# First block: the outgoing products of the second group of chunks by seven products for eight, a row of constants loaded later, casts placed behind copies, and two changes of places

## The chip, the cores and the metric

The kernel runs on one core of one Trainium2 chip. The metric is the time of one execution on the device in microseconds (us), smaller is better. The core has a matrix engine (PE), a vector engine (DVE), a scalar engine (ACT), a general engine (POOL, used here to issue DMAs that add to what lies in memory) and SyncE (SP, used to issue plain DMAs). A profile of one execution gives the start and duration of each engine's instructions.

## The reference

One layer of an encoder, 512 tokens of 1024 channels in fp32. Two SwiGLU blocks stand around a mixer:

```python
h = modulate(rmsnorm(x, norm_ffn1), sh1, sc1)
x = x + 0.5 * g1 * swiglu(h, w_ffn1_in, w_ffn1_out)      # first block
...                                                       # mixer: window attention and differential attention
h = modulate(rmsnorm(x, norm_ffn2), sh3, sc3)
x = x + 0.5 * g3 * swiglu(h, w_ffn2_in, w_ffn2_out)      # second block

def swiglu(h, w_in, w_out):
    gate, up = jnp.split(h @ w_in, 2, axis=-1)
    return (jax.nn.silu(gate) * up) @ w_out
```

The hidden width is 2816. The nine shifts, scales and gates (`sh1` ... `g3`) are 72 columns of 128 values, each a product of `silu(c)` with a part of `w_mod`; the kernel calls them columns of the modulation.

## The kernel before

**Layout.** The residual `x` is held as 8 tiles `x[m]` of 128 channels x 512 tokens. The hidden width is 22 chunks of 128, or 11 pairs `p` of two chunks. A product in fp32 is made of three matmuls: high part by high part, high by low, low by high. `split_from` makes the two parts: a cast on ACT (the high part) and a subtraction on DVE (the low part, line 189). Weights arrive by DMA in `raw` or `u4` buffers and are split into a place of two large tiles, `high` and `low`. `high_low` gives the place: five places in turn, each with an offset in words, the aside (16 for `ASIDE`, -8 for `FIRST`), so that an aside moves where in its place a weight begins.

**Two ways to multiply.** `mm3` (lines 173 to 175) makes plain products, 512 tokens wide in the outgoing products of the first block. A `Unit` multiplies two-by-two blocks with seven products in place of eight (the scheme of Strassen and Winograd). Its seven products are called `s1`, `a11`, `a12`, `s2`, `s3`, `s4` and `a22`; each is made by `two` (lines 457 to 459) from matmuls that are 256 tokens wide, one half of the tokens. Its weight sums come from DMAs on POOL that add one block of weights onto another in the buffer (`s1` from two blocks, `s2` from `s1`, `s4` from `s2`, `s3` from `a11`). `Unit.after` copies a finished bank (ACT, line 535), adds banks onto copies (DVE, lines 537, 542 and 545) and calls `post` with each quarter of the result.

**The first block.** Pairs 0 to 2 take their input products plainly, pairs 3 to 10 are Units of depth 4 (24 matmuls to each of the seven products); `in_post1` turns their results into activations: silu on ACT, then `silu(gate) * up` on DVE (line 885), then a split. The outgoing products are taken in four groups of chunks, `CHUNKS`: 0 to 5, 6 to 11, 12 to 15, 16 to 21. When the pairs of a group are done, an `Out1` follows: for each of the 8 outputs `m` all chunks of the group, 3 matmuls of 128x512 to a chunk, and an update of `x[m]` on DVE (line 946).

**What sets the order.** The items (one product of a Unit, or one output of an `Out1`) stand in a list, and the matrix engine runs them in that order (`run_items`). An item's weights are asked for (`ASK`) and split (`MAKE`) so many items ahead. `in_order` names the products whose split is tied behind the latest copy of a bank on ACT (`issue_after(copied[0])`). Beside each item `side1` adds 0.27 to a credit, and at 1.0 one column of the modulation is loaded and reduced on DVE (line 282). SP, POOL and DVE run their instructions strictly in the order given.

**The second block** runs Units for its input and its outgoing products alike: `act_split` makes the seven operands of an outgoing Unit from a pair's activations, piece by piece beside the items. It starts with `plain` (pair 0, plain blocks `a11`, `a21`, `a12`, `a22`, in two halves of the tokens), `lead` (pair 1) and `units[2]`.

## Time and profile before

| what | us |
|---|---|
| three timed runs | 1034.28, 1035.11, 1036.36 |
| their median | 1035.11 |
| the profiled execution, its whole time | 1038.52 |
| the profiled execution, span of its trace | 1036.7 |
| first block, first matmul of pair 3 | 81.62 |
| plain outgoing products, chunks 0 to 5 | 108.90 to 141.57 |
| plain outgoing products, chunks 6 to 11 (the second group) | 179.73 to 212.41 |
| plain outgoing products, chunks 12 to 15 | 250.56 to 272.36 |
| second block, first product of a Unit | 711.30 |

Starts are on the profiled execution's own clock, from the start of its span. The whole time of that execution is 1.8 us above its span, and 3.4 us above the median of the timed runs. The profile shows each matmul with a duration of its own; since matmuls overlap, the pace of the matrix engine is read from the distance between their starts.

### The profile page before, as it was taken

Reading aid. Unit: us, or ns where it says so; the run is one execution under the profiler, and the core shown is the slowest. Engines: PE = TensorE matmul, PEld = TensorE weight load, DVE = VectorE, ACT = ScalarE, POOL = GpSimd, SP = SyncE. Lnnn points to the kernel's source line nnn. Section 1 sums busy time; section 2 is a strip of 40 time slices with the busy share of each in tenths; the row PEclk is TensorE's granted clock in tenths of the full one; section 3 lists DMA queues with packets and bytes.
Section 4 is the critical chain, followed back from the end, with each engine's and each line's share of the span. In section 5 each row is a group of like instructions: output and inputs, shape, how many; then the busy total and the mean of one; then the engine's idle time right before and its main releaser. Section 6 shows DMA issues by size and latency. Waiting matters only on the chain.

```text
span 1036.7 us, 18849 instructions
## 1 busy us (share of the span) xinstructions
PE 1030.0 (99%) x7346; PEld 950.1 (92%) x7346; DVE 788.1 (76%) x1457; ACT 583.5 (56%) x1013; POOL 162.2 (16%) x189
## 2 busy tenths in 40 slices
PE   9999999999999999999999999999999999999998
PEld 6889899899998998899888888989999999999998
DVE  6987667567797679859772688976898777877877
ACT  6754335244455343668785856525867546654553
POOL 1101110110110100543323101001112112112210
PEclk9999999999999999999999999999999999999999
DMA  9978887967884359796737934974598998999974
GB/s 358 356 222 203 234 235 215 257 157 222 236 204 149 137 214 410 232 283 137 176 79 186 267 133 153 362 242 102 103 235 183 241 223 215 221 229 214 210 156 112
DMA packets 70233, 220.39 MB, mean 213 GB/s; under 512 B 8448, under 2 KB 13184, under 8 KB 70144
## 3 DMA queue, kind: packets, MB, share of 16 engines
q1 hardware_dynamic: 47808, 146.52, 39.1%
q0 software_dynamic: 19200, 68.17, 36.0%
q10 hardware_dynamic: 3136, 4.51, 1.2%
q8 instruction: 57, 0.93, 0.3%
q14 instruction: 32, 0.26, 0.1%
HBM read 208.94 MB, written 10.23 MB: 211 GB/s over the span
## 4 chain that ended last, share of the span: by engine, by line
PE 92%; DVE 2%; DMA 2%; ACT 2%; issue 1%; POOL 0%; DVEq 0%; SPq 0%; ACTq 0%
PE acc L457 7%; PE acc L458 7%; PE acc L459 7%; PE sc L459 6%; PE sc L457 6%; PE sc L458 6%; PE sc L174 5%; PE sc L173 5%; PE sc L175 5%; PE acc L173 4%; PE acc L175 4%; PE acc L174 4%; PE tp L1279 2%; PE acc L708 2%; PE acc L1201 2%; PE acc L1200 2%
## 5 line engine op out<-in xcount | busy, mean ns | idle before, releaser
L189 ACT CAST high<-raw 128x1024 fp32r<-128x1024 f32 (+2 forms) x176 | 158.4, 914 | 152.3 <-PE sc L174 40.8
L189 DVE TENSOR_TENSOR low<-raw,high 128x1024 fp32r<-128x1024 f32 (+2 forms) x176 | 183.4, 1051 | 39.7 <-ACT high L189 38.2
L457 PE MATMUL acc<-b,high 128*128 128x256 f32 x508 | 141.1, 278 | 0.0
L458 PE MATMUL acc<-b,high 128*128 128x256 f32 x508 | 140.8, 277 | 0.1
L459 PE MATMUL acc<-b,low 128*128 128x256 f32 x508 | 140.7, 277 | 0.0
L459 PE MATMUL sc<-b,low 128*128 128x256 f32 x500 | 138.4, 277 | 0.0
L457 PE MATMUL sc<-b,high 128*128 128x256 f32 x500 | 138.4, 277 | 0.0
L458 PE MATMUL sc<-b,high 128*128 128x256 f32 x500 | 138.4, 277 | 0.0
L189 ACT CAST high<-u 128x1024 fp32r<-128x1024 f32 (+1 forms) x73 | 75.5, 1034 | 53.8 <-PE sc L174 20.2
L189 DVE TENSOR_TENSOR low<-u,high 128x1024 fp32r<-128x1024 f32 (+1 forms) x73 | 87.7, 1201 | 21.6 <-ACT high L189 19.9
L174 PE MATMUL sc<-b,high 128*128 128x512 f32 (+1 forms) x272 | 97.2, 357 | 0.3 <-DVE b L189 0.3
L173 PE MATMUL sc<-b,high 128*128 128x512 f32 (+1 forms) x272 | 97.4, 358 | 0.0
L175 PE MATMUL sc<-b,low 128*128 128x512 f32 (+1 forms) x272 | 97.0, 357 | 0.0
L457 PEld LDWEIGHTS acc<-b,high 128*128 128x128 f32 x508 | 95.6, 188 | 0.4 <-ACT f L535 0.2
L458 PEld LDWEIGHTS acc<-b,high 128*128 128x128 f32 x508 | 95.4, 188 | 0.4 <-DVE b L1895 0.3
L459 PEld LDWEIGHTS acc<-b,low 128*128 128x128 f32 x508 | 95.4, 188 | 0.0
L457 PEld LDWEIGHTS sc<-b,high 128*128 128x128 f32 x500 | 94.2, 188 | 0.0
L458 PEld LDWEIGHTS sc<-b,high 128*128 128x128 f32 x500 | 93.9, 188 | 0.0
L459 PEld LDWEIGHTS sc<-b,low 128*128 128x128 f32 x500 | 93.8, 188 | 0.0
L173 PE MATMUL acc<-b,high 128*128 128x512 f32 (+1 forms) x240 | 89.1, 371 | 0.0
L175 PE MATMUL acc<-b,low 128*128 128x512 f32 (+1 forms) x240 | 86.5, 361 | 0.0
L174 PE MATMUL acc<-b,high 128*128 128x512 f32 (+1 forms) x240 | 86.5, 360 | 0.0
(397 smaller groups left out, 2715.4 us busy)
## 6 DMA issues: line engine op xcount, KB each, us to landing
u<-w_mod SPq DMA_DIRECT2D x38, 512.0 KB, 7.8
b<-w_mod SPq DMA_DIRECT2D x32, 512.0 KB, 5.9
raw<-w2i SPq DMA_DIRECT2D x31, 512.0 KB, 5.0
u<-w2i POOLq DMA_DIRECT2D x31, 512.0 KB, 6.5
raw<-w1u SPq DMA_DIRECT2D x24, 512.0 KB, 7.0
u<-w1u POOLq DMA_DIRECT2D x24, 512.0 KB, 7.5
raw<-w1o SPq DMA_DIRECT2D x24, 384.0 KB, 4.9
raw<-w_gate SPq DMA_DIRECT2D x16, 512.0 KB, 5.2
```

Of the source, the lines that this page charges most:

```text
L173: PE.matmul(out, wh, xh, start=first, stop=False)
L174: PE.matmul(out, wh, xl, start=False, stop=False)
L175: PE.matmul(out, wl, xh, start=False, stop=last)
L189: last = S.copy(hi, src), V.tensor_tensor(lo, src, f(hi), ALU.subtract)
L457: PE.matmul(out, wh[:, s], xh, start=first and j == 0, stop=False, skip_group_check=True)
L458: PE.matmul(out, wh[:, s], xl, start=False, stop=False, skip_group_check=True)
L459: PE.matmul(out, wl[:, s], xh, start=False, stop=last and j == 1, skip_group_check=True)
L708: PE.matmul(out1[i][:, r], w[:, i * P : (i + 1) * P], h[:, r], start=first and r.start == 0, stop=last and r.stop == T, skip_group_check=True,
L1200: PE.matmul(out[t][:, 0:n], hh[k][:, ht], wh[:, o : o + n], start=k == 0, stop=False)
L1201: PE.matmul(out[t][:, 0:n], hh[k][:, ht], wl[:, o : o + n], start=False, stop=False)
L1279: PE.transpose(tp[:, j * P : (j + 1) * P], src, ident)
```

## The change

It has six parts.

1. **The second group by sevens.** `SEVEN = (1,)`: chunks 6 to 11 (pairs 3, 4, 5) are no longer multiplied by an `Out1`, but by two outgoing Units of depth 3 (`out_unit1`, outputs 0 to 3 and 4 to 7). Their weights are laid out as `w1q`, 128x768 to a block. The activations of the three pairs are turned into seven operands each by `act_split`, which moves up from the second block and serves both.
2. **The order of items.** Units 4, 5 and 6 run first; the two outgoing Units then run interleaved with unit 6, with each other and with unit 7.
3. **Columns of the modulation.** The credit of an item is 0.6 for an output of a plain group, 0.25 for a product of a Unit and 0.1 beside the items of the sevens, for 0.27 before.
4. **The row of constants** (`row`, used after the first block) is loaded beside the first item of unit 9, not early; until then its `u4` buffer is free for others.
5. **Casts behind copies.** For the Units that follow a pair of the sevens (4, 5 and 6), the splits of five products are tied behind the latest copy (`s1`, `s2`, `s3`, `s4`, `a22`), for two before.
6. **Places.** `FIRST` stays on `s2` of units 4 and 8 and goes from unit 6. In the second block `a21` and `a22` of `plain` and `a11` of `units[2]` lie at `THIRD` (48); before they lay at the ordinary aside and at `FIRST`.

```diff
+THIRD = 48
...
-EARLY, NEXT, SIDE, LATER = 3, 3, 0.27, 4
+SEVEN, RATES = (1,), (0.6, 0.25, 0.1)
+EARLY, NEXT, LATER = 3, 3, 4
...
-    row = u4(F32).rearrange("p a b -> p (a b)")[:, 0:NROW]
     freq = keep([P, HD // 2], "freq")
     small_loads = [
-        (row, a["row"].partition_broadcast(P)), (kept[0], a["pos"]), (freq, a["freq"].partition_broadcast(P)),
+        (kept[0], a["pos"]), (freq, a["freq"].partition_broadcast(P)),
     ]
...
         g = u.v["g" + c[2]]
+        if u.p in by_sevens:
+            V.tensor_tensor(g, g, v, ALU.mult)
+            return
         V.scalar_tensor_tensor(g, g, -1.0, v, ALU.mult, ALU.mult)
+        if u.p in by:
+            return
...
-        u.p, u.in_order = p, ('s2', 's4')
+        u.p, u.in_order = p, ("s2", "s4")
+        if p - 1 in by_sevens:
+            u.in_order = ("s1", "s2", "s3", "s4", "a22")
...
-        elif 2 * p in [c.start for c in CHUNKS[1:]] or p == PLAIN + 1:
+        elif 2 * p in [CHUNKS[i].stop for i in range(len(CHUNKS) - 1) if i not in SEVEN] or p == PLAIN + 1:
             u.asides = {"s2": FIRST}
...
+    def act_split(u, k):
+
+        ta, tb = f2(), f2()
+        b = {f"b{n + 1}{t + 1}": u.v[f"g{t + 1}"][:, r] for t in range(2) for n, r in enumerate(HALVES)}
+        b.update(n1=ta[:, T1], n2=ta[:, T2], t3=tb[:, T1], t4=tb[:, T2])
+        for o in ("n1", "b11", "b21", "n2", "b22", "t3", "t4"):
+            if o in SUMS:
+                sub(b[o], *(b[q] for q in SUMS[o]), o in NEGATED)
+            act[o, k] = t = act_place()
+            split_from(*t, b[o])
+            yield
...
+    def out_unit1(part, g, odd):
+        def post(c, v, u):
+            n, t = int(c[1]) - 1, int(c[2]) - 1
+            for j in range(2):
+                m = 4 * g + 2 * n + j
...
+                w = (less if n == 0 else modv[G1])[:, m : m + 1]
+                if n == 0 and m not in negated:
+                    negated.add(m)
+                    V.tensor_scalar(w, modv[G1][:, m : m + 1], -1.0, None, ALU.mult)
+                xr = x[m][:, HALVES[t]]
+                V.scalar_tensor_tensor(xr, v[:, j * H : (j + 1) * H], w, xr, ALU.mult, ALU.add)
+
+        r = slice((part.start - PLAIN) * 2 * P, (part.stop - PLAIN) * 2 * P)
+        srcs = {q: a["w1q"][g, i][:, r] for i, q in enumerate(("a11", "a12", "a21", "a22"))}
+        u = Unit(srcs, len(part), act_operand, post, odd)
+        return u
+
+    def load_row():
+        rows.append(u4(F32).rearrange("p a b -> p (a b)")[:, 0:NROW])
+        nc.sync.dma_start(rows[0], a["row"].partition_broadcast(P))
+
+    by[-1] = lambda: (iter(()), 0, load_row)
...
+        for v, nxt in zip(order, order[1:] + [None]):
+            n = RATES[1 + (v.p in by_sevens or v not in units1.values())]
+            due = [v.p - 1] if v in units1.values() and v.p - 1 in by else []
+            if v is units1[NH - 2]:
+                due.append(-1)
...
+            item1(v, "s2", *due, n=n)
+            to = nxt is not None and v in units1.values() and nxt not in units1.values()
+            if nxt and not to:
+                item1(nxt, "s1", n=n)
+            item1(v, "s3", n=n)
+            item1(v, "s4", n=n)
+            if to:
+                item1(nxt, "s1", rest=True, n=n)
+            if nxt:
+                item1(nxt, "a11", n=n)
+            item1(v, "a22", n=n)
...
-    units[2].asides = {"a11": FIRST}
+    units[2].asides = {"a11": THIRD}
+    plain.asides = {"a21": THIRD, "a22": THIRD}
```

**On the matrix engine.** Before, unit 6's `a12` (bank `op`) was followed by the `Out1` of the second group, whose matmuls are 512 wide (bank `sc`, the first of 8 outputs). The names are output bank, then tokens operand and weights:

```order
L459 MATMUL op_165_1698<-b8_13_98,low_94 128x256
L457 MATMUL op_165_1698<-b8_13_98,high_87 128x256
L458 MATMUL op_165_1698<-b8_15_100,high_87 128x256
L459 MATMUL op_165_1698<-b8_13_98,low_94 128x256
L173 MATMUL sc_167_1729<-b8_122_983,high_87 128x512
L174 MATMUL sc_167_1729<-b8_122_983,high_87 128x512
L175 MATMUL sc_167_1729<-b8_122_983,low_94 128x512
```

Now unit 6 goes on. Shown are the last three matmuls of its `s2` (bank `acc_167`), six of its `s4` (bank `acc_163`), and the first three of its `s3`, which adds to the bank of `s2` again:

```order
L461 MATMUL acc_167_1663<-b8_103_732,high_87 128x256
L462 MATMUL acc_167_1663<-b8_103_732,high_87 128x256
L463 MATMUL acc_167_1663<-b8_103_732,low_94 128x256
L461 MATMUL acc_163_1566<-b8_13_98,high_87 128x256
L462 MATMUL acc_163_1566<-b8_15_100,high_87 128x256
L463 MATMUL acc_163_1566<-b8_13_98,low_94 128x256
L461 MATMUL acc_163_1566<-b8_13_98,high_87 128x256
L462 MATMUL acc_163_1566<-b8_15_100,high_87 128x256
L463 MATMUL acc_163_1566<-b8_13_98,low_94 128x256
L461 MATMUL acc_167_1663<-b8_104_739,high_87 128x256
L462 MATMUL acc_167_1663<-b8_104_739,high_87 128x256
L463 MATMUL acc_167_1663<-b8_104_739,low_94 128x256
```

In the other units the 24 matmuls of the next unit's `s1` stand between `s2` and `s3`; at this one place (`to` in the code) only six matmuls of `s4` stand there, and the copy of bank `acc_167` has to be made within them. The same arrangement stands in both kernels in unit 10, which has no next unit.

**On ACT**, before, the copy of unit 6's `a11` (from `acc_162`) stood ahead of the plain group, with the casts of that group's weights (`raw` to `high`, 768 wide) behind it:

```order
L877 ACTIVATE f2_157_1542<-f2_157_1542 128x512
L189 CAST b8_160_1630<-f2_157_1542 128x2x256
L535 COPY f2_163_1665<-acc_162_1640 128x512
L189 CAST high_87<-raw_161_1635 128x768
L189 CAST high_87<-raw_164_1696 128x768
```

Now the copy for unit 6's `s3` (`f2_175` from `acc_167`) stands behind a silu, a cast of an activation's operand and a cast of an outgoing Unit's weights:

```order
L880 ACTIVATE f2_168_1688<-f2_168_1688 128x512
L193 CAST b8_176_1798<-f2_171_1731 128x256
L193 CAST high_87<-raw_165_1626 128x768
L539 COPY f2_175_1793<-acc_167_1663 128x512
L193 CAST high_87<-raw_169_1693 128x1024
```

What moved: ahead of the copy there is now a cast of weights, which waits for its weights' DMA.

**On DVE**, before, each output of the plain group brought one split of weights (`low`, 768 wide) and one update of `x` (512 wide):

```order
L189 TENSOR_TENSOR low_94<-raw_168_1751,high_87 128x768
L189 TENSOR_TENSOR low_94<-raw_170_1778,high_87 128x768
L946 SCALAR_TENSOR_TENSOR x_3_78<-sc_167_1729,mod2_90,x_3_78 128x512
L189 TENSOR_TENSOR low_94<-raw_173_1805,high_87 128x768
L946 SCALAR_TENSOR_TENSOR x_4_79<-sc_169_1756,mod2_90,x_4_79 128x512
L189 TENSOR_TENSOR low_94<-raw_175_1829,high_87 128x768
```

Now a product of the outgoing Units brings a split of the same width; each quarter of a result brings a sum of banks (L546, L541) and two updates of 256 (L992):

```order
L546 TENSOR_TENSOR f2_182_1920<-f2_182_1920,tp_185_1952 128x512
L193 TENSOR_TENSOR low_94<-raw_177_1867,high_87 128x768
L992 SCALAR_TENSOR_TENSOR x_3_78<-f2_182_1920,sm_79_572,x_3_78 128x256
L992 SCALAR_TENSOR_TENSOR x_4_79<-f2_182_1920,sm_79_572,x_4_79 128x256
L193 TENSOR_TENSOR low_94<-raw_183_1922,high_87 128x768
L193 TENSOR_TENSOR low_94<-u4_170_1728,high_87 128x768
L541 TENSOR_TENSOR f2_180_1897<-f2_180_1897,sc_181_1901 128x512
L992 SCALAR_TENSOR_TENSOR x_5_80<-f2_180_1897,mod2_90,x_5_80 128x256
L992 SCALAR_TENSOR_TENSOR x_6_81<-f2_180_1897,mod2_90,x_6_81 128x256
```

What moved: the updates of `x` are twice as many and half as wide, and sums of banks and splits of more weights stand among them. Over the program PE has 7240 rows for 7132, DVE 1448 for 1401, ACT 898 for 875 and POOL 192 for 184; SP has 330 in both. From the end of unit 10 on, the order of each engine is the same in both kernels.

185 lines of the change are left out of this document (104 added, 81 removed).

## The prediction

> **What bounds the kernel now.** I read the page first, then the waits of the matrix engine, then starts in the timeline. The page's head:
>
> ```profile
> span 1036.7 us, 18849 instructions
> PE 1030.0 (99%) x7346; PEld 950.1 (92%) x7346; DVE 788.1 (76%) x1457; ACT 583.5 (56%) x1013; POOL 162.2 (16%) x189
> PEclk9999999999999999999999999999999999999999
> PE 92%; DVE 2%; DMA 2%; ACT 2%; issue 1%; POOL 0%; DVEq 0%; SPq 0%; ACTq 0%
> ```
>
> The matrix engine is busy for 99% of the span at its full granted clock, and 92% of the chain that ended last is its work. What it waits for (longest first and last):
>
> ```profile
> PE acc L633 <- DVE sm L639: 0.9, 1, 0.9
> ...
> PE acc L708 <- ACT b L695: 0.3, 1, 0.3
> ```
>
> Columns are total, number and longest wait. There are five such rows, 2.6 us together, and none has a line of the seven-product code (gaps of some tenths show only in the starts, below). So time is saved by fewer or denser matmuls, and lost where another engine comes late. Busy time does not give a matmul's cost, since matmuls overlap; their starts do. Around the stage that is replaced:
>
> ```profile
> 179.62 0.28 PE L459 MATMUL op<-b,low 128*128 128x256 f32 x1
> 179.73 0.40 PE L173 MATMUL sc<-b,high 128*128 128x512 f32 x1
> 179.96 0.40 PE L174 MATMUL sc<-b,high 128*128 128x512 f32 x1
> ```
>
> Start, duration, instruction. The last narrow start (256 columns) is 0.11 us ahead of the next, the first wide one (512) 0.23. Over stretches, in the windows:
>
> ```profile
> 179.73:212.41 32.68, 32.68 (x147) 27.03 (x146) 17.93 (x26) 7.13 (x8) 3.52 (x4) 1.00 0.91 258
> 212.41:215.20 2.79, 2.79 (x25) 2.79 (x24) 0.75 (x1) 0.00 (x0) 0.00 (x0) 1.00 0.00 0
> 142.00:180.00 38.00, 38.00 (x336) 37.96 (x335) 28.86 (x38) 21.27 (x28) 3.50 (x4) 1.00 0.84 233
> 142.00:251.00 109.00, 109.00 (x816) 103.30 (x815) 75.77 (x100) 49.43 (x65) 11.43 (x13) 1.00 0.78 214
> 766.00:820.00 54.00, 54.00 (x462) 54.00 (x462) 46.63 (x73) 35.42 (x57) 9.17 (x11) 1.00 0.91 225
> ```
>
> After the length stand PE, PEld, DVE, ACT and POOL busy with their counts, the granted clock, the DMA share and GB/s; a count takes in the two or three matmuls that run over an edge. The first row is the whole stage that is replaced: 8 outputs x 6 chunks x 3 = 144 wide matmuls in 32.68 us, 226.9 ns each. In the third row some 335 narrow ones fill 38 us: 113.4 ns, half of it. I use 113.3.
>
> **The change, part by part.**
>
> *The sevens.* Two outgoing Units x 7 products x 3 pairs x 2 x 3 = 252 narrow matmuls, 252 x 0.1133 = 28.55 us, for 32.68: **-4.1 us**. The 24 matmuls from 212.41 to 215.20 (second row), the first after wide ones, took 2.79 us for 24 x 0.1133 = 2.72; unit 6 no longer follows wide ones: **-0.1**.
>
> *The new wait.* Unit 6's `s3` follows `s2` after only six matmuls. Unit 10 has that order in the kernel before (matrix engine, then ACT):
>
> ```profile
> 313.69 0.28 PE L458 MATMUL acc<-b,high 128*128 128x256 f32 x1
> 313.80 0.28 PE L459 MATMUL acc<-b,low 128*128 128x256 f32 x1
> 314.07 0.39 PE L457 MATMUL acc<-b,high 128*128 128x256 f32 x1
> 314.30 0.28 PE L458 MATMUL acc<-b,high 128*128 128x256 f32 x1
> 314.42 0.28 PE L459 MATMUL acc<-b,low 128*128 128x256 f32 x1
> ```
>
> ```profile
> 313.44 0.59 ACT L535 COPY f<-acc 128x512 f32<-128x512 f32 x1 [1.02 <-PE acc L459]
> ```
>
> The starts 313.80, 314.07, 314.30 are 270 and 230 ns apart for 113: 0.27 us lost to a copy that was issued at once. In unit 6 a cast of 768 stands ahead of the copy, 0.84 us by its row below; bounds are 0 (the copy lands within the six) and 0.27 + 0.84 = 1.1. I take the nearest row, **+0.3**. Behind the copy on ACT stand casts for later items, not this one.
>
> *What hides the rest.* Costs on DVE and ACT:
>
> ```profile
> L189 DVE TENSOR_TENSOR low<-raw,high 128x768 fp32r<-128x768 f32 x32 | 30.1, 953 | 9.2 <-ACT high L189 9.2
> L189 DVE TENSOR_TENSOR b<-f,b 128x256 fp32r<-128x256 f32 x71 | 27.9, 420 | 2.1 <-ACT b L189 1.6
> L189 DVE TENSOR_TENSOR b<-f,b 128x512 fp32r<-128x512 f32 x22 | 15.1, 688 | 5.2 <-ACT b L189 5.2
> L588 DVE SCALAR_TENSOR_TENSOR f<-f,f 128x256 f32<-128x256 f32 x22 | 9.2, 420 | 0.1
> L545 DVE TENSOR_TENSOR f<-f,acc 128x512 f32<-128x512 f32 x12 | 8.2, 683 | 1.8 <-PE acc L459 1.7
> L946 DVE SCALAR_TENSOR_TENSOR x<-sc,mod,x 128x512 f32<-128x512 f32 x24 | 18.0, 750 | 27.1 <-PE sc L175 27.1
> L1818 DVE SCALAR_TENSOR_TENSOR x<-f,mod,x 128x256 f32<-128x256 f32 x36 | 15.8, 481 | 0.5
> L282 DVE CUSTOM_DVE_ANT_0 u<-u,ka 128x1024 f32<-128x1024 f32 x15 | 18.2, 1218 | 0.0
> L189 ACT CAST high<-raw 128x768 fp32r<-128x768 f32 x32 | 26.0, 837 | 24.5 <-PE sc L174 11.5 <-DMA raw<-w1o 7.1 <-PE acc L458 3.2
> ```
>
> Off DVE go 8 splits of 768 (7.6), 8 updates (6.0) and 6 splits of 512 (4.1): 17.7 us. On it come 14 splits of 768 (13.3), 21 splits and 12 sums of 256 (33 x 0.420 = 13.9), 6 sums of banks (4.1) and 16 updates of 256 (7.7): 39.0. Net +21.3. The columns there are ten before, two instructions each:
>
> ```profile
> 142.00:251.00 109.00, 12.44 (x20) 1.00 0.78 214
> ```
>
> By the new rates eight remain, -2.5 (the two come later, beside stages with room). The row 142 to 251 has 75.8 us of DVE in 109; it becomes 94.6 in 105, 90%. That is close, but the row 766 to 820, which runs sevens throughout, has 46.6 of 54, 86%. ACT gets 6 casts of 768, 6 copies, and 21 casts of 256 for 6 of 512, some 13 us on 49: 60%. Both lie beside matmuls: I cost them at **0**, and in the rivals as the price if that cover goes.
>
> *Transfers.* SP's 8 loads of 384 KB become 8, POOL gets 8 more that add, in the same 105 us:
>
> ```profile
> raw<-w1u SPq DMA_DIRECT2D x24, 512.0 KB, 7.0
> u<-w1u POOLq DMA_DIRECT2D x24, 512.0 KB, 7.5
> raw<-w1o SPq DMA_DIRECT2D x24, 384.0 KB, 4.9
> ```
>
> 214 GB/s x 109 us is 23.3 MB; with 3.1 MB more in 105 us it is 252 GB/s, and the share rises from 0.78 to about 0.9, as in the row 766 to 820. **0** again.
>
> *The row of constants* is one more load in SP's row beside unit 9; behind it stand loads that are asked for six to nine products (16 to 24 us) before use and land in 7.0 us. On DVE a copy from it stands ahead of a split for unit 10; if the row is late, DVE waits up to a landing, about 7 us, against a need more than 8 us off. **0**. Its buffer is free until then, which can only help. *Casts behind copies* keep copies early in the stretch of the sevens and are part of that cover.
>
> *Places.* The narrow matmuls do not always go at 113 ns. At the start of the second block, again in windows:
>
> ```profile
> 729.69:741.00 11.31, 11.31 (x99) 11.31 (x98) 9.76 (x19) 8.79 (x16) 0.91 (x1) 1.00 0.29 46
> 741.00:743.87 2.87, 2.87 (x26) 2.87 (x25) 2.60 (x3) 2.87 (x4) 0.86 (x1) 1.00 0.02 6
> 743.87:746.68 2.81, 2.81 (x27) 2.81 (x25) 2.81 (x4) 1.68 (x4) 0.86 (x1) 1.00 0.99 163
> 746.68:765.75 19.07, 19.07 (x171) 19.02 (x169) 17.78 (x27) 13.94 (x24) 4.35 (x5) 1.00 1.01 216
> ```
>
> By the code these are `plain`'s second half (96 matmuls), `s1` of `lead` (24), `a11` of `units[2]` with `FIRST` (24), and seven more products (168): 117.8, 119.6, 117.1 and 113.5 ns each. If `THIRD` brings all to 113.3 it gives 0.43 + 0.15 + 0.09 = 0.7 us. If it runs at the slowest pace of these rows, 119.6, and leaves 117.8 behind it up to 765.75, it costs 96 x 0.0018 + 24 x 0.0025 + 168 x 0.0045 = 0.2 + 0.1 + 0.8 = 1.1. From 766 to 820 there are at most 462 in 54 us, where 54 / 0.1133 = 477 would fit: 15 fewer, 1.7 us, of which another phase at the start may be rid. So -2.4 to +1.1; both signs are open, I take **0**.
>
> Sum: -4.1 - 0.1 + 0.3 = **-3.9 us**. Against the profiled execution, 1038.5, that is 1034.6. It stands 3.4 us above the median of the timed runs; from 1035.1 it is **1031.2 us**.
>
> **A rule against it.** The rows say that one wide matmul costs two narrow ones (226.9 to 113.1). The Trainium skill, "TensorE: Matmul & The Clock Gate", section "Back-to-back issue gap", gives streams of weight load and matmul about 131 ns for 512 columns and 81 for 128; on a line between them 256 columns would be some 98, an estimate, and the stage would go from 18.9 to 24.7 us, slower by 5.8. The rows here contradict both its figures and its ratio.
>
> **The rivals.**
>
> 1. *The new wait leaves a slower pace.* From 766 on (the row above) the matmuls were slow, 54 / 460 = 117.4 ns, for as long as the window; after 314.30 the next start came 0.12 us later. If unit 6's wait does the first, 558 narrow matmuls up to the next wide stage take 4.5 ns more: 2.5 us, **1033.7**, no measurable change. For it: slow stretches exist at a granted clock of 1.00, so the clock does not undo them. Against: unit 10, the same arrangement, was back at once. Chance 0.2.
> 2. *DVE comes late in the sevens.* At 90% over 105 us it has 10 us of room, but not evenly; a column (1.2 us) ahead of a split can delay an item by as much. Two or three such waits cost 2 to 3 us: **1033.7**. Chance 0.12.
> 3. *Slower: a landing is exposed.* An outgoing Unit's `s4` weights are `s2`'s with a block added by POOL. `s2` is split four products ahead of its own, and `s4` comes three after that; at 18 x 0.1133 = 2.04 us a product, not 2.72, these seven are 14 us for a landing of 7.5, a cast and a split. If landings stretch past 14 us, each late one is waited for in full; from 6.0 us (3.9 + 0.2% of the time) the kernel is slower. One landing exposed: 1031.2 + 7.5 = **1038.7**. For it: share 0.9, 8 more adding transfers. Against: 766 to 820 runs the same chain at 0.91 and the list of waits has no DMA. Chance 0.08.
> 4. *A narrow matmul costs more than half a wide one*, because its weight load shows. Were all exposed,
>
> ```profile
> L457 PEld LDWEIGHTS acc<-b,high 128*128 128x128 f32 x508 | 95.6, 188 | 0.4 <-ACT f L535 0.2
> ```
>
> 252 x 0.188 = 47.4 us for 32.7: +14.7, **1049.8**. The rule above, of the Trainium skill, would come from such a cost. The starts at 113 speak against it: chance 0.02.
>
> **How the numbers follow.** The forecast has 0.58. The range takes in its open terms: down by 0.3 (no wait) and 2.4 (places), to 1028.5; up by rival 1 or 2 and 1.1 (places), to 1034.8. Rivals 3 and 4 stay outside. A measurement of this kernel can tell 0.2%, 2.1 us, from no change, so faster is below 1033.0: the forecast, and a part of rivals 1 and 2 where places help, 0.70. Within 0.2%: 0.20. Slower: rivals 3 and 4, 0.10.
>
> **What would show it.** In the profile after: no matmul of 512 columns between units 5 and 7, and narrow ones at 113 ns in their place; the span of the first block shorter by 3.9 us; a gap of 0.3 us behind `s2` of unit 6, and the pace behind it (rival 1); waits of PE on DVE or ACT lines in the sevens (rival 2) or on `raw<-w1q` (rival 3). The second block's start shows the places by 96 and 24 matmuls as above. It is wrong if the first block gains under 2 us, or if the time changes behind 820, where nothing is altered.

## The result and the profile after

The changed kernel takes 1045.73 us in the median of six runs (1045.16 to 1050.21), the kernel before beside it 1034.89 us (six runs, 1034.28 to 1036.36). The ratio is **1.0102, with a 95% interval of 1.0086 to 1.0117**: 1% slower, where 0.4% faster was forecast. The profiled execution of the changed kernel has a span of 1045.0 us, for 1036.7.

The page's head after the change, the same lines as shown of before:

```profile
span 1045.0 us, 19171 instructions
PE 1029.7 (99%) x7454; PEld 954.7 (91%) x7454; DVE 805.2 (77%) x1508; ACT 593.9 (57%) x1040; POOL 169.2 (16%) x197
PEclk9999999999999999999999999999999999999999
```

The matrix engine is busy for 1029.7 us, as long as before, although it was given less to do; its share still rounds to 99%. The list of its waits shows what the share hides. Columns: engine, bank and line, what was waited for, then total, number and longest in us.

```profile
PE acc L461 <- ACT f L539: 3.9, 2, 2.9
PE acc L461 <- DVE f L541: 3.1, 1, 3.1
PE acc L637 <- DVE sm L643: 0.9, 1, 0.9
PE sc L461 <- ACT f L539: 0.8, 1, 0.8
PE tp L463 <- DVE low L193: 0.6, 1, 0.6
PE acc L463 <- DVE low L193: 0.5, 1, 0.5
```

Before, no row of this list had a line of the seven-product code. Now five of the first six have (L461 and L463 are the former L457 and L459): copies of banks on ACT, a sum of banks on DVE, the splits of weights on DVE.

Windows give the place. Each row has the stretch and its length, then PE, PEld, DVE, ACT and POOL busy with counts, the granted clock, the DMA share and GB/s. First the kernel before, from the first matmul of pair 3 to the first wide one of the last group:

```profile
81.62:321.68 240.06, 240.06 (x1730) 224.80 (x1728) 172.51 (x241) 106.43 (x140) 25.79 (x30) 1.00 0.79 216
```

The changed kernel, the same stretch of the program, then the stretch around the sevens, three pieces at unit 6, and one of the second block:

```profile
80.54:328.72 248.18, 240.15 (x1837) 229.30 (x1836) 189.29 (x291) 117.45 (x167) 32.88 (x38) 0.99 0.84 224
...
142.00:251.00 109.00, 105.50 (x911) 104.90 (x910) 85.50 (x131) 59.89 (x89) 18.50 (x21) 0.98 0.89 223
...
181.00:185.80 4.80, 1.50 (x11) 1.10 (x9) 4.33 (x9) 2.92 (x8) 0.00 (x0) 1.00 0.89 246
185.80:190.30 4.50, 4.44 (x24) 4.44 (x25) 3.54 (x8) 2.05 (x4) 0.87 (x1) 0.62 0.83 259
190.30:217.50 27.20, 27.20 (x242) 27.20 (x241) 22.30 (x34) 12.94 (x19) 6.20 (x7) 1.00 0.99 236
...
766.00:820.00 54.00, 52.96 (x452) 52.76 (x451) 49.21 (x81) 37.11 (x62) 10.94 (x13) 1.00 0.89 208
```

The stretch grew by 8.12 us (248.18 - 240.06) where 3.9 less was forecast, so 12.0 us were lost in it. It began 1.08 us earlier (80.54 for 81.62), which lies ahead of what was changed on the matrix engine (in the profiles below it begins anywhere from 79.67 to 80.85), and what follows the stretch adds 1.2; -1.1 + 8.1 + 1.2 is within 0.1 of the 8.3 us between the spans.

The sevens themselves run at the pace forecast: the row from 190.30 holds 242 matmuls in 27.20 us, 240 x 0.1133. What was lost lies in two places. I measure each by the starts of the matmuls: the sum of what their distances exceed 113.3 ns (226.7 for wide ones). **At unit 6's `s3`** (178 to 192 us) it is 5.5 us: the row from 181.00 has PE busy for 1.50 of 4.80 us, and the row behind it ran at a granted clock of 0.62, with matmuls 213 ns apart for a while ("half a clock" below). **At units 8 and 9** (from the third plain group to ahead of unit 10's own wait, 273 to 320 us) it is 6.0 us. The rest of the stretch has 1.4, where the kernel before has 0.7 in all.

**Who is late at unit 6.** The timeline of ACT (start, duration, instruction, and in brackets the idle time before it and who ended it), changed kernel:

```profile
174.45 0.83 ACT L193 CAST high<-u 128x768 fp32r<-128x768 f32 x1 [5.15 <-DMA u<-w1q]
...
180.66 1.02 ACT L193 CAST b<-f 128x256 fp32r<-128x256 f32 x3 [0.94 <-DVE f L889]
183.52 0.63 ACT L880 ACTIVATE f<-f 128x512 f32<-128x512 f32 x1 [1.84 <-DVE f L546]
...
185.23 0.58 ACT L539 COPY f<-acc 128x512 f32<-128x512 f32 x1
```

The last row is the copy that `s3` waits for; `s2` had ended at 181.5, and `s3` started at 185.86. ACT had stood idle for 5.15 us, ten us earlier, for the weights of an outgoing Unit (`u<-w1q`) that nothing on PE needed yet. DVE stood behind it, and later ACT behind DVE:

```profile
175.32 0.96 DVE L193 TENSOR_TENSOR low<-u,high 128x768 fp32r<-128x768 f32 x1 [3.47 <-ACT high L193]
...
181.00 1.22 DVE L193 TENSOR_TENSOR low<-u,high 128x1024 fp32r<-128x1024 f32 x1
...
182.80 0.68 DVE L546 TENSOR_TENSOR f<-f,op 128x512 f32<-128x512 f32 x1
```

The DMA that ended ACT's 5.15 us is the one that adds on POOL. It was issued 8.8 us before that cast could start, and stood on POOL behind another adding DMA that had waited 12 us for its buffer, while SP had issued the plain load that it adds to at 149.41 already:

```profile
165.13 0.88 POOL L516 DMA_DIRECT2D raw<-w1u  x1 [12.02 <-DVE low L193]
165.68 1.23 POOL L497 DMA_DIRECT2D u<-w1q  x1
```

So three queues that run in order hand the lateness on: POOL to ACT (5.15), ACT to DVE (3.47), DVE to ACT (1.84), ACT to PE.

**Who is late at units 8 and 9.** The row of constants and the weights of unit 9's `s1` in the timeline of the changed kernel (SP, ACT and DVE):

```profile
263.39 0.47 SPq L495 DMA_DIRECT2D u<-w1u  x1
...
273.79 0.38 SPq L1003 DMA_DIRECT2D u<-row  x1
...
282.58 1.05 ACT L193 CAST high<-u 128x1024 fp32r<-128x1024 f32 x1 [4.99 <-DMA u<-w1u]
...
285.55 0.17 DVE L1257 COPY sink<-u 128x8 f32<-128x8 f32 x1 [6.70 <-DMA u<-row]
...
289.22 0.68 DVE L541 TENSOR_TENSOR f<-f,acc 128x512 f32<-128x512 f32 x1
```

and before:

```profile
255.27 0.51 SPq L491 DMA_DIRECT2D u<-w1u  x1
```

DVE waits 6.70 us for the row of constants, which landed 11.7 us after its issue; the sum L541, which frees a bank, stands behind, and PE waits 3.1 us for it. ACT meanwhile waits 4.99 us for the adding DMA of unit 9's `s1`; SP had issued the plain load below that sum at 263.39, 12.1 us after the start of the third plain group (251.25), before 4.7 us after it.

The transfers by queue from 142 to 251 us, with packets, MB and the share of 16 DMA engines' time (software_dynamic is POOL's adding DMAs, hardware_dynamic SP's loads), before:

```profile
q1 hardware_dynamic: 5190, 16.44, 41.1%
q0 software_dynamic: 1872, 6.82, 36.5%
```

and after:

```profile
q0 software_dynamic: 2962, 9.71, 52.0%
q1 hardware_dynamic: 4608, 14.42, 36.0%
```

A MB of the adding DMAs takes 52.0/9.71 = 5.4% of the stretch, one of SP's loads 36.0/14.42 = 2.5%. Without the adding DMAs (`e13_no_adds`, below) SP's loads `raw<-w1u` land after 3.6 us in the median, not 6.1. The Trainium skill, "DMA: Bandwidth & Descriptors", section "Issuing engines are not separate DMA queues", says that DMAs issued from different engines end on the same 16 DMA engines and interleave. These landings agree with it.

### The profile page after: what moved, and what is told of

Same layout as the page of the kernel before. It is cut to its first block, busy times and chain, and to the rows that moved or that the text cites. A ratio compares the mean times of both kernels' runs of the same rounds, so it can differ in the third digit from the quotient of the medians.

```text
span 1045.0 us, 19171 instructions
## 1 busy us (share of the span) xinstructions
PE 1029.7 (99%) x7454; PEld 954.7 (91%) x7454; DVE 805.2 (77%) x1508; ACT 593.9 (57%) x1040; POOL 169.2 (16%) x197
## 5 line engine op out<-in xcount | busy, mean ns | idle before, releaser
L461 PE MATMUL acc<-b,high 128*128 128x256 f32 x542 | 151.8, 280 | 7.1 <-ACT f L539 3.9
L463 PE MATMUL acc<-b,low 128*128 128x256 f32 x542 | 151.4, 279 | 0.5 <-DVE low L193 0.5
L462 PE MATMUL acc<-b,high 128*128 128x256 f32 x542 | 151.2, 279 | 0.4 <-DVE b L2010 0.4
L461 PE MATMUL sc<-b,high 128*128 128x256 f32 x534 | 148.0, 277 | 0.8 <-ACT f L539 0.8
L463 PE MATMUL sc<-b,low 128*128 128x256 f32 x534 | 147.9, 277 | 0.0
L462 PE MATMUL sc<-b,high 128*128 128x256 f32 x534 | 147.8, 277 | 0.0
L193 ACT CAST high<-u 128x1024 fp32r<-128x1024 f32 (+1 forms) x79 | 80.4, 1018 | 57.2 <-PE sc L462 12.1
L461 PEld LDWEIGHTS acc<-b,high 128*128 128x128 f32 x542 | 102.7, 189 | 8.0 <-ACT f L539 4.6
L463 PEld LDWEIGHTS acc<-b,low 128*128 128x128 f32 x542 | 102.8, 190 | 0.8 <-DVE low L193 0.7
L462 PEld LDWEIGHTS acc<-b,high 128*128 128x128 f32 x542 | 102.6, 189 | 0.7 <-DVE b L2010 0.6
L461 PEld LDWEIGHTS sc<-b,high 128*128 128x128 f32 x534 | 100.3, 188 | 1.0 <-ACT f L539 1.0
L463 PEld LDWEIGHTS sc<-b,low 128*128 128x128 f32 x534 | 100.5, 188 | 0.0
L462 PEld LDWEIGHTS sc<-b,high 128*128 128x128 f32 x534 | 100.3, 188 | 0.0
L177 PE MATMUL sc<-b,high 128*128 128x512 f32 (+1 forms) x224 | 78.7, 352 | 0.0
L178 PE MATMUL sc<-b,high 128*128 128x512 f32 (+1 forms) x224 | 78.5, 351 | 0.1
L179 PE MATMUL sc<-b,low 128*128 128x512 f32 (+1 forms) x224 | 78.4, 350 | 0.0
```

The lines of the kernel that those rows point to most:

```text
L177: PE.matmul(out, wh, xh, start=first, stop=False)
L178: PE.matmul(out, wh, xl, start=False, stop=False)
L179: PE.matmul(out, wl, xh, start=False, stop=last)
L193: last = S.copy(hi, src), V.tensor_tensor(lo, src, f(hi), ALU.subtract)
L461: PE.matmul(out, wh[:, s], xh, start=first and j == 0, stop=False, skip_group_check=True)
L462: PE.matmul(out, wh[:, s], xl, start=False, stop=False, skip_group_check=True)
```

## The experiments

The timed ratio is to the kernel before, with its 95% interval. Block is the stretch of the first block as above, and the next columns are the excess of starts at unit 6 (178 to 192 us) and at units 8 and 9 (up to unit 10's own wait); these three come from one profiled execution each, in us.

| run | median (range) | ratio (95%) | block | unit 6 | units 8, 9 |
|---|---|---|---|---|---|
| before | 1034.89 | 1 | 240.06 | 0.0 | 0.1 |
| after | 1045.73 (1045.16 to 1050.21) | 1.0102 (1.0086 to 1.0117) | 248.18 | 5.5 | 6.0 |
| e1_copy_late | 1041.09 (1039.88 to 1045.12) | 1.0054 (1.0034 to 1.0074) | 243.76 | 5.3 | 2.1 |
| e2_s4_first | 1043.13 (1040.28 to 1044.04) | 1.0059 (1.0034 to 1.0083) | 248.06 | 4.1 | 5.8 |
| e3_both | 1039.31 (1037.05 to 1044.19) | 1.0037 (1.0020 to 1.0053) | 244.08 | 1.7 | 5.3 |
| e4_places_back | 1045.88 (1044.00 to 1046.42) | 1.0087 (1.0062 to 1.0113) | 249.01 | 4.8 | 5.9 |
| e5_before_row_late | 1036.69 (1035.52 to 1040.10) | 1.0008 (0.9996 to 1.0021) | 241.36 | 0.0 | 1.4 |
| e6_out_weights_later | 1044.86 (1041.06 to 1046.27) | 1.0078 (1.0053 to 1.0103) | 250.00 | 5.2 | 5.6 |
| e7_old_rates | 1042.92 (1041.28 to 1043.10) | 1.0066 (1.0048 to 1.0083) | 243.56 | 6.7 | 0.1 |
| e8_all_four | 1041.50 (1040.93 to 1045.12) | 1.0059 (1.0036 to 1.0081) | 244.21 | 4.6 | 0.1 |
| e9_s4_split_late | 1045.66 (1044.29 to 1046.72) | 1.0088 (1.0058 to 1.0118) | 250.22 | 5.4 | 6.4 |
| e10_two_causes_gone | 1042.15 (1037.58 to 1044.49) | 1.0058 (1.0039 to 1.0077) | 244.98 | 4.2 | 2.1 |
| e11_next_s1_between | 1039.89 (1038.47 to 1042.86) | 1.0036 (1.0022 to 1.0050) | 244.21 | 0.0 | 1.8 |
| e12_all_but_sevens | 1036.71 (1034.33 to 1039.24) | 1.0009 (0.9999 to 1.0019) | 244.14 | 0.0 | 4.2 |
| e13_no_adds | 1034.02 (1032.14 to 1035.81) | 0.9988 (0.9979 to 0.9997) | 238.99 | 0.8 | 1.0 |
| e14_less_dve | 1045.16 (1043.70 to 1048.57) | 1.0101 (1.0085 to 1.0118) | 250.31 | 5.5 | 5.8 |
| e15_neither | 1031.97 (1030.88 to 1033.86) | 0.9966 (0.9955 to 0.9978) | 236.18 | 0.3 | 0.1 |
| e16_places_alone | 1035.25 (1034.79 to 1036.72) | 1.0002 (0.9994 to 1.0011) | 240.06 | 0.0 | 0.1 |
| e17_no_out_adds | 1040.43 (1038.30 to 1042.12) | 1.0039 (1.0026 to 1.0052) | 242.69 | 0.4 | 5.3 |
| e18_no_out_adds_old_rates | 1038.29 (1034.15 to 1042.19) | 1.0018 (1.0000 to 1.0037) | 240.19 | 2.6 | 1.2 |

One profile says only so much: `e2` and `e3` have the same order of work up to unit 6 and lose 4.1 and 1.7 us there, and in `e4`, `e9`, `e11`, `e12` and `e14` the profiled execution is the slowest of those timed. The block ends where the last plain group begins; the five runs with 0.25 of a column beside a plain output (`e7`, `e8`, `e10`, `e11`, `e18`) lose 1.0 to 2.3 us more right behind it, where three or four of the columns that were put off stand on DVE.

### Single waits: the copy behind the row, the order at unit 6, the places

**e1_copy_late.** The copy from the row of constants, with what follows from it, is tied behind the last split of the first block.

```diff
-    V.tensor_copy(
-        sink.rearrange("p (g k) -> p k g", k=2), row[:, ROW_SINK : ROW_SINK + 8].rearrange("p (k g) -> p k g", k=2)
-    )
+    with tc.issue_after(split[1]):
+        V.tensor_copy(
+            sink.rearrange("p (g k) -> p k g", k=2), row[:, ROW_SINK : ROW_SINK + 8].rearrange("p (k g) -> p k g", k=2)
+        )
```

> The changed kernel with one thing moved: the copy of the sink values out of the row of constants stands on DVE behind the last weight split of the first block, not in the middle of unit 8. The row is loaded at the same place. Theory (head of line: DVE stood for 6.7 us on the row, and the sum L541 that unit 8's a22 needs stood behind it): the waits of the matrix engine between 281 and 303 us, about 5 us with the slower pace behind them 6.6 us, go; 1045.7 becomes about 1039. Rival (the row's own transfer slows the weights' loads, and DVE has too little time there anyway): less than 2 us goes.

The wait of 3.1 us for the sum L541 is gone; 0.95 us at 297.4 and a pace of 118 ns behind it are left. Unit 6 is unchanged. The row still lands late (11.4 us after its issue); that DVE stood for it was the first cause of the waits at units 8 and 9. The time is 2 us above the theory's.

**e2_s4_first.** Unit 6's `s4` ahead of its `s3`, so that 24 matmuls and not six stand between `s2` and `s3`.

```diff
-            item1(v, "s3", n=n)
-            item1(v, "s4", n=n)
+            for q in ("s4", "s3") if to else ("s3", "s4"):
+                item1(v, q, n=n)
```

> The changed kernel with unit 6's s4 ahead of its s3, so that 24 matmuls (2.72 us) stand between s2 and s3 where there were six (0.68 us). Theory (the copy that s3 waits for stands on ACT behind two casts and a silu that wait for a late DVE): 2.0 of the 3.8 us of waiting go, and with a shorter idle stretch the 1.7 us at a lower granted clock behind it too; 1045.7 becomes 1042 to 1043. Rival (DVE lacks the time in the sevens as a whole): the wait comes back at the next products, 1045 or more.

Unit 6 loses 4.1 us instead of 5.5: the copy comes so late that 24 matmuls don't cover it either. The few matmuls between `s2` and `s3` are not the whole cause; they are the place where the lateness shows.

**e3_both.** Both edits together.

> Both edits together. Theory: the two waits are apart (100 us between them), so their gains add: 1045.7 - 6.6 - 3.5 = 1035 to 1036. Rival (one backlog of DVE runs through both): clearly less than the sum of the two.

Unit 6 falls to 1.7 us, and no half clock follows; the waits at units 8 and 9 return without the row: 2.6 us at 283.3, then half a clock. ACT stands 7.54 us idle there for the adding DMA of `u<-w1u`. A wait that is taken away uncovers the next one. The gains did not add up, as the theory had it: 1039.31 for 1035 to 1036.

**e4_places_back.** `a21`, `a22` of `plain` and `a11` of `units[2]` at their places of before.

```diff
-    units[2].asides = {"a11": THIRD}
-    plain.asides = {"a21": THIRD, "a22": THIRD}
+    units[2].asides = {"a11": FIRST}
```

> The changed kernel with the places at the start of the second block as before (a11 of units[2] at FIRST, a21 and a22 of plain at the ordinary aside). Theory (the places speed up plain's matmuls by 0.7 us, and a copy on ACT that waits for DVE 20 us later takes that back): no change, 1045.7 within 0.7 us, with the wait at 770 us shorter by about what the matmuls ahead of it lose. Rival (the places cost something by themselves): 1.2 us faster.

No change outside the intervals: the places carry none of the loss that can be measured.

**e5_before_row_late.** The kernel before, with the row of constants loaded beside unit 9 and nothing else.

```diff
-    row = u4(F32).rearrange("p a b -> p (a b)")[:, 0:NROW]
...
-        (row, a["row"].partition_broadcast(P)), (kept[0], a["pos"]), (freq, a["freq"].partition_broadcast(P)),
+        (kept[0], a["pos"]), (freq, a["freq"].partition_broadcast(P)),
...
+    def load_row():
+        rows.append(u4(F32).rearrange("p a b -> p (a b)")[:, 0:NROW])
+        nc.sync.dma_start(rows[0], a["row"].partition_broadcast(P))
+        side1()
```

> The kernel before with one part of the change alone: the row of constants is loaded beside the first product of unit 9. Theory (the copy from the row stands on DVE ahead of unit 8's sums and waits for the row's landing, which took 11.7 us in the changed kernel): the matrix engine waits behind the third plain group, 2 to 5 us, 1035 becomes 1037 to 1040. Rival (the row costs only together with the new rates of columns, which make the loads ahead of it late): within 1 us of before.

One wait of 1.1 us at 279 us, and a ratio that can't be told from 1. The late row is not free, but it takes the company of the other parts to cost three us.

### Moving weights and columns about

**e6_out_weights_later** splits the first outgoing Unit's `s1` weights three items ahead and not five, so that the cast on which ACT waited comes later. **e7_old_rates** loads 0.25 of a column beside a plain output and not 0.6. **e8_all_four** has e1, e2, e6 and e7 together.

```diff
+        if g == 0:
+            u.MAKE = {**Unit.MAKE, "s1": 3}
...
-SEVEN, RATES = (1,), (0.6, 0.25, 0.1)
+SEVEN, RATES = (1,), (0.25, 0.25, 0.1)
```

> The changed kernel with the split of the first outgoing Unit's s1 weights made three products ahead, not five; on ACT its cast moves from row 132 to row 136, behind a silu and a copy. Theory (ACT stood 5.2 us on the landing of that Unit's summed weights, with the silu, the activations' casts and at last the copy for unit 6's s3 behind it): the 3.8 us of waiting at 181 us shrink to 1 us or less, and the 1.7 us at a lower clock behind it go; 1045.7 becomes 1040 to 1041.5. Rival (DVE is simply full in the sevens): the wait stays above 2.5 us, 1044 or more.

> The changed kernel with 0.25 column for each output of a plain group, not 0.6 (0.25 and 0.1 elsewhere as changed). Theory (five loads of w_mod in the third plain group hold up SP ahead of unit 9's weights, whose load was issued 12 us after that group's start for 5 us before): the wait of ACT on u<-w1u at 277 us shrinks from 5.0 us to under 2, the waits of the matrix engine at 284 us and after lose 2 to 4 us; 1045.7 becomes 1042 to 1044. Rival (the row alone makes the waits): no change.

> The changed kernel with four edits: the copy from the row late, unit 6's s4 ahead of its s3, the first outgoing Unit's s1 split three products ahead, 0.25 column for each output of a plain group. Theory (the seven-product stage itself saves its 4.1 us, and all that was lost are transfers waited for at the head of in-order engines): 1031 to 1034, faster than before. Rival (DVE lacks time in the sevens): 1036 or more.

In e6 ACT no longer waits for `w1q`; it waits 3.03 us for the next weights, unit 6's own `s4`, and unit 6 loses 5.2 us as before. In e7 the waits at units 8 and 9 are gone (0.1 us): SP issued the plain load for unit 9's `s1` at 257.42, the row landed 7.5 us after its issue, and DVE waited 1.31 us for it. So columns between SP's loads are part of that cause. But unit 6 loses 6.7 us, and one more wait of 1.3 us comes at 346.6, where columns that were put off are now due. In e8 none of the four edits gets rid of unit 6's wait: ACT stands 4.64 us for unit 6's `s4` weights.

**e9_s4_split_late** splits unit 6's `s4` one item ahead and not two. **e10_two_causes_gone** has that with e6 and e7. **e11_next_s1_between** has e6 and e7 with the first outgoing Unit's `s1` put between unit 6's `s2` and `s3`, as in every other unit.

```diff
+        if p - 1 == by_sevens[-1]:
+            u.MAKE = {**Unit.MAKE, "s4": 1}
...
-            if nxt and not to:
-                item1(nxt, "s1", n=n)
+            if nxt:
+                item1(nxt, "s1", rest=to, n=n)
...
-            if to:
-                item1(nxt, "s1", rest=True, n=n)
```

> The changed kernel with unit 6's s4 split one product ahead, not two: on ACT its cast then stands behind the copy that unit 6's s3 waits for, where it stood ahead of it. Theory (that cast waits for the landing of s2's weights with a block added, 9.1 us after POOL's issue, and ACT, in order, holds the silu, the activations' casts and the copy behind it): the 3.8 us at 181 us shrink to 1 us, the lower clock behind them goes; 1045.7 becomes 1040 to 1041. Rival (DVE full; the copy is late by other ways too): 3 us or more of waiting stay, 1044 or more.

> The changed kernel with three edits: unit 6's s4 split one product ahead, the first outgoing Unit's s1 split three ahead, 0.25 column for each output of a plain group. Theory (the rates make the waits behind the third plain group, the two casts those in the sevens): all waits above 1 us in the first block go, but the columns left over come at its end (1.3 us there with the old rates); 1032.5 to 1035, at least level with before. Rival: above 1037.

> As the run with three edits, but with the first outgoing Unit's s1 (18 matmuls, 2.0 us) between unit 6's s2 and s3 in place of the later split of s4. Theory: the copy for s3 gets 2.0 us of matmuls as cover and the cast of s4's weights comes behind it, so no wait at s3; but s1's operand of pair 5 has 2.7 us less to be made, which may give a wait of up to 1.5 us ahead of that s1; 1032 to 1035. Rival (DVE full): the operand is late by 2 us or more, 1037 or more.

In e9 ACT waits 5.72 us for `w1q` as in the changed kernel. In e10 it waits 1.90 us for the same weights, and the copy still comes late. In e11 unit 6 loses nothing, but the block is as long as in e8: 1.8 us at 199.9, 1.0 at 226.0, 1.3 at 278.9, and 2.0 with half a clock behind it at unit 10. In e10 and e11 DVE still waits for the row (4.17 and 4.90 us), although they have the rate of e7. The theories of e6 and e8 to e11 all missed, by 3 us or more, and their rivals, a full DVE in all but e10, had the number right; whether they had the cause, only e14 below can tell. That each of these edits moves the wait and none removes the loss points to a shortage that they all share. The next runs ask of what.

### What is short: the sevens, the adding DMAs, or DVE

**e12_all_but_sevens.** The second group plainly, as before; row, rates and places as in the changed kernel.

```diff
-SEVEN, RATES = (1,), (0.6, 0.25, 0.1)
+SEVEN, RATES = (), (0.6, 0.25, 0.1)
```

> The second group is multiplied plainly again, as before (eights); the late row of constants, the new rates of the columns and the places of the second block stay as in the changed kernel. My theory (the sevens make the wait at unit 6's s3 and save 4.1 us by themselves; the rate of 0.6 beside plain outputs, with the late row, makes the waits at unit 8 and 9): no wait of matmuls and no half clock from 180 to 195 us; with plain groups also at 0.6 in the second group, the columns stand between the loads there too, so 2 to 7 us of waits are left, by 284 us or earlier, and the time is 1037 to 1042 us, ratio 1.002 to 1.007. Rival (all of the loss hangs on the sevens, which fill DVE and the transfers, and the other parts cost only in their company): no wait over 0.5 us in the first block, and the time is that of before, 1034.5 to 1036 us, ratio within 0.002 of 1.

Unit 6 is free of waits. At units 8 and 9 there is one, with half a clock behind it, 4.2 us in all; DVE waits for the row:

```profile
279.86 0.17 DVE L1257 COPY sink<-u 128x8 f32<-128x8 f32 x1 [7.37 <-DMA u<-row]
```

Both theories miss a half: the waits are there, yet the time is 1.0009 of before. The profile gains 1.9 us back in the second block (below), and it is of the slowest of the twelve executions, so that the typical one need not lose 4.2 us. Without the sevens the other parts cost at most 0.2%; with them, 1.0%.

**e13_no_adds** leaves out all 40 adding DMAs of the first block's Units, **e14_less_dve** 28 instructions on DVE, **e15_neither** both.

```diff
-                G.dma_start(t, self.srcs[src], accum_op=ALU.add)
+                if self.adds:
+                    G.dma_start(t, self.srcs[src], accum_op=ALU.add)
...
-                V.scalar_tensor_tensor(xr, v[:, j * H : (j + 1) * H], w, xr, ALU.mult, ALU.add)
...
-            if o in SUMS:
+            if o in SUMS and u not in units1.values():
                 sub(b[o], *(b[q] for q in SUMS[o]), o in NEGATED)
+            elif o in SUMS:
+                b[o] = b[SUMS[o][0]]
```

> All 40 adding DMAs of the first block's Units are left out (the products are then made of plain weights, so the output differs); every split, copy, sum and matmul stays, in the same places. Theory L (landings): ACT's casts wait for an adding DMA that lands 8 to 10 us after its issue, and what stands behind them comes late. Then the waits at unit 6's s3 (5.5 us with the half clock) and at units 8 and 9 (6.7 us) go, each to under 1 us, and the time is 1034 to 1037 us, ratio 0.999 to 1.002. Theory D (DVE has no room: 94.6 us of work in 105): the waits stay within 30 per cent, ratio over 1.007.

> The 16 updates of x behind the outgoing Units of the second group and the 12 sums of activations' operands in the first block are left out (x gets no part of chunks 6 to 11, and the operands that are sums are plain blocks, so the output differs): 16 x 0.48 + 12 x 0.42 = 12.7 us less on DVE; all transfers and matmuls stay. Theory L: the wait at unit 6's s3 comes before any of the 16 updates and after some of the sums; it stays within 1 us of 5.5 us, and the ratio stays over 1.006. Theory D: both groups of waits shrink to under half, ratio under 1.004.

> Both are left out (adding DMAs of the first block's Units, and the 28 DVE instructions). Theory L: as without the adding DMAs alone, within 2 us. Theory D: as with the lighter DVE alone, within 2 us. If each takes a part: below both, 1030 to 1034 us, where the 4.1 us of the sevens are to be seen.

The list of waits of e14, in the first block, has the long rows of the changed kernel, with 12.7 us less on DVE:

```profile
PE acc L461 <- ACT f L539: 3.5, 2, 2.7
PE acc L461 <- DVE f L541: 3.5, 1, 3.5
PE acc L463 <- DVE low L193: 0.4, 1, 0.4
```

Windows of e13, the block and the stretch around the sevens:

```profile
80.41:319.40 238.99, 238.75 (x1837) 228.72 (x1836) 188.50 (x291) 117.04 (x166) 0.56 (x1) 1.00 0.47 156
...
142.00:251.00 109.00, 108.91 (x929) 108.02 (x928) 89.41 (x137) 61.95 (x91) 0.00 (x0) 1.00 0.43 139
```

DVE has 188.50 us to do in it, as in the changed kernel (189.29), in 9.2 us less time; the DMA share fell from 0.89 to 0.43, and unit 6 loses 0.8 us, units 8 and 9 1.0. The row still comes late and the columns still stand between SP's loads, and it costs little: the row is there 7.2 us after its issue and DVE waits 1.68 us for it, not 6.70. With e14 this bears the landing theory out, and that of a full DVE falls. DVE's load counts once the landings are on time: e15 has 2.8 us less than e13. The block of e15:

```profile
80.12:316.30 236.18, 236.18 (x1838) 226.31 (x1836) 178.45 (x263) 116.59 (x166) 0.56 (x1) 1.00 0.48 158
```

236.18 - 240.06 = -3.88 us: the gain of the sevens, in full. (What the kernel before would gain without its own adding DMAs wasn't tried; its block has 0.7 us of excess to give.)

**e16_places_alone.** The kernel before with `THIRD` at the three products of the second block.

```diff
-    units[2].asides = {"a11": FIRST}
+    units[2].asides = {"a11": 48}
+    plain.asides = {"a21": 48, "a22": 48}
```

> The kernel before with the two changes of places only. If the start of the second block then keeps the pace of 113.3 ns from about 768 to 820 us, as in the run of all parts but the sevens, the profile gains 1.0 to 2.0 us there and the time is 1033 to 1035 us, ratio 0.998 to 1.000. If the pace of 117.8 ns hangs on a late copy near 768 us and not on the places, it is as before, ratio within 0.001 of 1.

```profile
766.00:820.00 54.00, 54.00 (x478) 54.00 (x477) 47.72 (x76) 35.54 (x56) 10.43 (x12) 1.00 0.92 223
```

478 matmuls in this window for 462 before: the whole stretch at 113 ns. The time is that of before all the same (1.0002). Over all profiled executions this stretch runs either at 117.8 ns (nine of twenty) or at 113.3 (ten), e5 partly at each; of those with the places of before, the kernel before is of the first kind and e4 of the second. So the pace isn't bound to the places alone, and what it is worth in timed runs can't be read from one profile. Bound to the places are the 96 matmuls of `plain`'s second half: 113.9 ns in every profile with `THIRD`, 117.8 in the three without (the kernel before, e4, e5).

### The change's own eight adding DMAs

**e17_no_out_adds** leaves out only those of the two outgoing Units. **e18_no_out_adds_old_rates** has in addition 0.25 of a column beside a plain output.

```diff
         u = Unit(srcs, len(part), act_operand, post, odd)
+        u.adds = False
         return u
```

> Only the 8 adding DMAs of the two outgoing Units of the second group are left out (their products are made of plain weights, so the output differs); the 32 of the other Units of the first block stay. If the 8 new ones make the wait at unit 6's s3: it goes from 5.5 us to under 1 us, the waits at units 8 and 9 (284 to 328 us) stay over 4 us, and the time is 1038 to 1041 us, ratio 1.003 to 1.006. If the 32 count as much: the wait at unit 6's s3 stays over 3 us, and the ratio over 1.006.

> As the one ahead, and beside the plain outputs 0.25 of a column to an item in place of 0.6. If the two waits are two causes (the 8 adding DMAs for unit 6, the columns for units 8 and 9): both go, no wait of matmuls over 1 us in the first block but unit 10's (0.9 to 1.5 us in the runs with this rate), 1032 to 1036 us, ratio 0.998 to 1.001. If a wait only moves on: over 4 us of waits are left in the first block, ratio over 1.003.

e17 is as its first theory said: unit 6 loses 0.4 us, units 8 and 9 5.3, at 1.0039. In the order of the changed kernel the eight adding DMAs of the outgoing Units are what makes unit 6 late. e18 is a miss in its stricter half: units 8 and 9 are down to 1.2 us, but unit 6 loses 2.6. ACT shows why, in e18:

```profile
177.46 1.05 ACT L193 CAST high<-u 128x1024 fp32r<-128x1024 f32 x1 [3.13 <-DMA u<-w1u]
```

It waits for the adding DMA of unit 6's own `s4`, one of the 32 that the kernel had before. With fewer adding DMAs the room is larger, but an order that uses it up elsewhere brings the wait back. Its first block is within 0.2 us of before, its timed median 1.9 us above the kernel before beside it (ratio 1.0000 to 1.0037); the profile has 2.3 us more behind the block, with this wait among them, while two columns stand on DVE ahead of the update of `x`:

```profile
PE sc L177 <- DVE x L384: 1.5, 1, 1.5
```

## Why the prediction was wrong

**The step that failed is "Transfers", set at "0 again".** The share of about 0.9 was measured (0.89), but by luck: 26.4 MB at 252 GB/s were forecast for it and 24.3 MB at 223 measured, and the share came out because a MB of the new adding DMAs takes twice the engines' time. What followed from it was wrong. The step compared with the row of 766 to 820 us, which has a share of 0.91 and no wait; that the other stretch holds such a share does not show that this one does. Nor were the 8 new adding DMAs like the 8 loads that they came beside: by time of the DMA engines a MB of them takes twice as much as one of SP's (5.4% and 2.5% of the stretch), and those on POOL are issued in order behind adding DMAs that wait for their buffers. Without the 40 adding DMAs the 12.0 us go to 2.8, without them and the 28 DVE instructions to nothing; without the eight new ones unit 6's 5.5 go to 0.4. Median landings hardly changed (SP's `raw<-w1u` 6.3 and 6.1 us before and after, POOL's `u<-w1u` 7.5 and 7.8, the longest of these 8.6 and 10.9); whether the engines' time or the place on POOL's queue counts for more, no run separates.

**Rival 3 had the resource, and the wrong road and size.** It asked whether an outgoing Unit's weights land before PE needs them, 14 us against 7.5, and gave it 0.08. They did land before. But ACT and DVE run in order: a cast that nobody needed for several us yet, and whose weights had not landed, held up a copy of another unit's bank. The margin to look at was not that of the weights but that of whatever stands behind the cast on its engine. The prediction looked at the row ahead of the copy, and priced it by its duration; the wait lay some rows earlier, and reached the copy by way of DVE.

**The new wait, +0.3, bounds 0 to 1.1.** In e15 the three starts at that place are

```profile
181.52 0.28 PE L463 MATMUL acc<-b,low 128*128 128x256 f32 x1
181.79 0.38 PE L461 MATMUL acc<-b,high 128*128 128x256 f32 x1
182.01 0.29 PE L462 MATMUL acc<-b,high 128*128 128x256 f32 x1
```

270 and 220 ns for 113, 0.27 us in all: the term was right where ACT is on time. In the changed kernel it was 3.8 us of waits and 1.7 of half clock. The upper bound was no bound: it assumed that ACT reaches the cast in time.

**The row of constants, 0.** The wait of DVE was forecast up to 7 us and was 6.70; "against a need more than 8 us off" was false. Behind the copy stood the sum L541, which PE waited for. The landing, 11.7 us, was sized by other loads' 7.0. Alone it costs nothing that can be measured (e5), in company about 4 us by the profiles (e1 takes 6.0 to 2.1; e12 has 4.2).

**The columns, beside stages with room.** There is room on DVE in the third plain group, but not on SP: the columns' loads wait for their place there, and unit 9's load stands behind them. e7 takes that cause away (6.0 to 0.1 us) and pays 2.0 us behind the block; e13 makes it harmless.

**The sevens, -4.1, and -0.1 behind them.** Right: 240 matmuls at 113.3 ns in the row from 190.30, and the block of e15 is 3.88 us shorter for a sum of 3.9. Rival 4 is out. The rule of the Trainium skill, "TensorE: Matmul & The Clock Gate", section "Back-to-back issue gap", that went with it is out too: the narrow matmuls took 113.3 ns, not the estimated 98.

**Work on DVE and ACT, 0.** DVE got 16.8 us more in the block (189.29 - 172.51), for 21.3 - 2.5 = 18.8 forecast; only 85.5 us of its work lies in the stretch from 142 to 251 us, where 94.6 were put. The cover held: rival 2 is not the cause (e14). It has its share of 2.8 us only where the landings are gone (e13 to e15).

**The places, 0.** Within 0.1% (e16). In its profile `plain`'s second half gained 0.4 us (113.9 ns for 117.8), and the 192 matmuls from `a11` of `units[2]` on lost 0.5, most of it in two short waits.

**Rival 1, a slower pace behind a wait,** exists, at 118 ns: behind the wait at 301.7 us up to the next wide stage, and from 774 to 819 us, where the changed kernel had waited 1.2 us for a copy (the kernel before had this pace there too, so it adds nothing to the difference; the wait does). It did not come where the rival put it: behind unit 6 the pace was 113.3 ns as soon as the clock was back.

The sign was wrong because two terms that were set at 0, transfers and the row with the columns, were some 11 of the 12.0 us, each by a road over engines that PE does not wait for directly.

## What to carry to other kernels

Before a transfer is costed at nothing, look up what stands behind its first reader on the reader's engine: an early cast that waits for late weights delays everything behind it, needed or not, and on in-order engines such waits add up from queue to queue. Reckon adding DMAs by their engines' time, here twice that of plain loads for a MB, and look at their place on the issuing queue; bytes alone hide both. When waits move about under edits and the sum stays, leave out the use of a whole resource once: here three such runs told what eleven moves had not.

## What the runs showed of the hardware

**A wait of the matrix engine can cost more than its length.** After the wait at unit 6 of the changed kernel, 17 matmuls came slower, 15 of them at 213 ns, and the granted clock was 0.62 over 4.5 us: 1.7 us more. The distance between the two starts around the wait was 3.1 us there. The same drop followed distances from 2.1 us (unit 10 in e11) to 3.9 us (at 286.8 us in e4). None followed 1.7 and 1.9 us (e3, e11), nor 2.5 us (unit 6 in e18), nor 3.3 us (at 286.6 us in the changed kernel). The Trainium skill, "TensorE: Matmul & The Clock Gate", section "Why this matters for your kernels", has the clock fall after idle gaps of over about 3 us. Here shorter gaps had the drop, and the one of 3.3 us had not. Section "What's actually happening" of that page of the Trainium skill says that the window in which the gate counts runs freely, and gives 1.2 GHz for the low state. From its cold gap of N / 1.2 ns, in section "Back-to-back issue gap", 213 ns for 256 columns is an estimate. The 213 ns measured agree with it. That the same length sometimes has the drop and sometimes not would fit a window that runs freely, which no run here tests by itself.

**The landing time of SP's loads hangs on POOL's adding DMAs.** From 142 to 251 us the median of SP's `raw<-w1u` is 6.1 us in the changed kernel, 4.4 without the eight new adding DMAs (e17) and 3.6 without all 40 (e13), but 6.3 in the kernel before, which has none of the eight; the row of constants took 11.7, 11.3 and 7.2 us in those three runs.

Left open: why the stretch of 766 to 820 us holds a DMA share of 0.92 without waits (e16), and what sets off the pace of 118 ns there.
